# Groups 2 to 7 instead of 2 to 6 of the up-projection in seven products, and the weight sums' transfers in a list that is not emptied ahead of the last gate

## The chip, the cores and the metric

The kernel runs on one core of one Trainium2 chip. The metric is the device time of one execution in microseconds (us). TensorE is called PE here, its weight loads PEld, VectorE DVE, ScalarE ACT, GpSimd POOL and SyncE SP, as in the profile.

## The reference, cut to what matters

The program computes two layers of an encoder trunk for 512 tokens of 1024 channels. Each layer has a mixing half and a feed-forward half:

```
h = rmsnorm(x)                          # per token
proj = h @ w_in                         # gates, convolution branch, three attentions
branch = [y_a, y_b, y_c, y_d] @ w_branch
mixed = sum_n sigmoid(gate_n) * branch_n
x = x + mixed @ w_out
u = depthwise_conv3(rmsnorm(x) @ w_up)  # 1024 -> 2 x 2816
x = x + (silu(u_gate) * u_up) @ w_down  # 2816 -> 1024
```

All arithmetic is float32. The change touches how `@ w_up` is split into products, and when some sums of weights for `@ w_down` and `@ w_up` are made.

## The kernel before, in words

**Float32 products.** Each weight tile of 128x1024 numbers is fetched from HBM to `w_raw` (L248, a DMA on SP's queue), rounded to `w_hi` on ACT (L252), and the rest is put into `w_lo` on DVE (L254). A product of such a pair with a pair `xh`, `xl` takes three matmuls, `w_hi*xh`, `w_hi*xl` and `w_lo*xh` (L273 to L275 in `prod`). A tile that has been fetched and split is a unit. `unit()` asks for units two ahead of the one that it hands out; there are three buffers each for `w_hi` and `w_lo`, and for the units of seven products four for the raw data (two named `w_raw`, two named `w_more`).

**The stages of a layer.** First come the token-major projections of the attentions, with the attentions and the convolution done step by step beside the PE's later products; then the gates of four branches in the order 1, 2, 3, 0 (`gates`, from L839). Each gate has eight blocks of 24 matmuls 128x512 and eight small branch products of 6. After the block of a gate, DVE makes `t` (L849), ACT the tanh (L851), and after the branch product DVE makes another `t` (L878); POOL adds it to the running sum `mx` (L879, for the last gate only for the blocks 0 to 5). In the last gate, branch 0, ACT and DVE then split the sum into `mh` and `ml` (L883, L884) for the product with `w_out`. The tiles `t` share two buffers (tag `t1`), so a third `t` waits until POOL has added the first. After `w_out` comes the feed-forward half: the up-projection (`ffn`), and the down-projection (`down`).

**Seven products.** The 44 blocks of 128 columns of the up-projection form 11 groups (gate and up columns of two neighbouring blocks). A whole group takes four blocks of 24 matmuls 128x512 (L273 to L275). For the groups in `SEVEN` a scheme of Strassen's kind takes seven products of 24 matmuls 128x256 each (L992 in `seven`): A11, A22 and A12 use a quarter of the weights as it is, S1 to S4 use sums of quarters, which the kernel makes itself in DRAM. S4 of a group is issued after the first product of the next group. The down-projection is done in seven products throughout and uses sums of weights too.

**The sums.** Two generators make them with DMAs from POOL's queue, DRAM to DRAM, some of them accumulating: `quarter_sums` (eight transfers of 512 KB for each group in `SEVEN`, L1110 by way of the helper `dma`) and after it `weight_sums` (24 transfers of 1024 or 768 KB for each layer, L1133 by way of `add`). Each of these DMAs waits for the matmul that was issued last when it was emitted (`paced`). They are chained in `slowly`, which makes 12 empty steps first, then one step for each transfer of `quarter_sums` and four for each of `weight_sums`.

**Side work.** `tick()` takes one step of every generator in the list `side`. A block of a gate ticks twice, a product of the seven twice. Ahead of the last gate, `layer` runs `while self.side: self.tick()`: the list is emptied there, with no matmul between the ticks. In the kernel before, the list holds the chain of sums as well. POOL takes its instructions in order, DMA issues and adds alike.

**Splits for the down-projection.** `split_pair` makes from two finished blocks of the up-projection the operands of the seven products of the down-projection. `EARLY` lists after which blocks the first six calls are emitted; the other five are emitted in `down`. The blocks of group 7 are 14 and 15.

Of the kernel before, what the change touches and what calls it, by code (L numbers as in the profile page):

```python
# [34 lines left out]

SLOW = 1

SEVEN = (2, 3, 4, 5, 6)


def up_steps():

    steps, held = [], []
    for g in range(NP2):
        if g in SEVEN:
            own = [('seven', g, n) for n in ('S3', 'A11', 'A22', 'S2', 'A12', 'S1', 'S4')]
        else:
            own = [('whole', 2 * g + i, s) for i in range(2) for s in range(2)]
        steps += own[:1] + held
        held = own[-1:] if g in SEVEN else []  # L50
        steps += own[1:len(own) - len(held)]
# [2 lines left out]

UP_STEPS = up_steps()

EARLY = (14, 15, 16, 18, 19, 20)
EPS = 1e-6
BIG = 1e30
EB = 4  # L60
# [35 lines left out]
def weight_units():  # L96
# [17 lines left out]
    for g in range(NP2):  # L114
        if g in SEVEN:
            units.extend(('quarter', (g, r, c), 1024) for r in range(2) for c in range(2))
# [102 lines left out]
class Trunk:  # L219
# [667 lines left out]
    def tick(self):  # L887

        for g in list(self.side):

            with self.tc.issue_after(self.last_mm.ins):
                r = next(g, 'end')
            if r == 'end':
                self.side.remove(g)
            if r in ('end', 'free') and g is self.head:
                self.head = None
                self.activate()
        return bool(self.side)

    def activate(self):  # L900
# [124 lines left out]
    def conv_part(self, i, s):  # L1025
# [22 lines left out]
        self.F.append(fl)  # L1048
        if i in EARLY:
            self.split_pair(self.F, EARLY.index(i), self.got)  # L1050

# [56 lines left out]
    def quarter_sums(self, l):  # L1108

        dma = lambda *a, **k: self.paced(self.nc.gpsimd.dma_start(*a, **k))  # L1110
        q, t = self.quarters[l], self.qsums[l]
        for g in SEVEN:
            for n in ('S1', 'S2', 'S3', 'S4'):
                t[g, n] = self.dram.tile([P, 1040], F32, name=f"q{n}{g}", tag=f"q{n}{g}", bufs=2)[:, :1024]
        for n, a in (('S3', (1, 0)), ('S1', (1, 1))):
            for g in SEVEN:
                dma(t[g, n], q[(g,) + a])
                yield
        for n, a in (('S3', (0, 0)), ('S1', (1, 0))):
            for g in SEVEN:  # L1120
                dma(t[g, n], q[(g,) + a], accum_op=ALU.add)
# [38 lines left out]
    def pair_tags(self, j):  # L1160
# [4 lines left out]
        late = [(f"lt{n // 2}", n % 2) for n in range(10)]  # L1165
        hi = [f"fh{2 * j}", f"fh{2 * j + 1}"] if j < len(EARLY) else x[2 * (j - len(EARLY)):][:2]
        lo = ["lo", "lo"] if j == 0 else [(f"fp{j - 1}", 0), (f"fp{j - 1}", 1)]
# [9 lines left out]
    def split_pair(self, F, j, got):  # L1177
# [19 lines left out]
        bh, bl = (t[:, (lo, hi)[j % 2]] for t in got['b'])  # L1197
        a = self.fp.tile([P, S], F32, name="sum", tag="xr" if j < len(EARLY) else "fth", bufs=2)

# [16 lines left out]
    def down(self, F, last):  # L1216
# [9 lines left out]

        got, todo = self.got, list(range(len(EARLY), NP2))
        A, B = ([self.mm() for _ in range(2)] for _ in range(2))
# [94 lines left out]
    def run(self):  # L1323
        nc, tc = self.nc, self.tc
        with ExitStack() as st:
# [36 lines left out]
            self.w_emitted = self.w_used = 0  # L1362
            self.first_hi = None
            self.w_ready, self.w_fast = [], 0
            self.side, self.waiting, self.head = [], [], None

            self.cst = self.const.tile([P, NRES], F32, name="cst", tag="cst", bufs=1)
            self.ident = self.cst[:, C_ID:C_ID + P]
# [40 lines left out]
    def layer(self, l):  # L1409
        tc = self.tc  # L1410
        last = l == L - 1
        self.Y, self.mixed, self.MH, self.glu_u = [None] * 4, [], [], []
        with tc.tile_pool(name="gate", bufs=1, reuse_waits="tile") as self.gp:
            with tc.tile_pool(name="attn", bufs=1, reuse_waits="tile") as self.ap:
                self.scratch = lambda: self.gp.tile([P, S], F32, name="raw", tag="t1", bufs=2)
                pss = self.token_major(None, self.aux) if l == 0 else self.early
                Q = self.new_Q()
                for b in range(NB):
                    self.evac_q(Q)(b, pss[b])
                with self.first():  # L1420
                    for _ in self.qk_stats(Q, 4, 4, None):
                        pass
                self.derive_params()
                V = self.new_V()
                self.tabs = [None] * 4
                self.queue(chain(self.na_biases(l, 3 if l else 5), self.qk_norm(Q, 4, 4, 0),
                                 self.attention('na', V, 1)))
                self.side.append(self.slowly(chain(self.quarter_sums(l), self.weight_sums(l))))
                Vd = self.new_V()
                self.project_v(V, Vd)  # L1430
                Q = self.project_qk()
                ready = self.beside(self.qk_stats(Q, 4, 4, 0))
                self.queue(chain(ready, self.qk_norm(Q, 4, 4, 2), self.attention('dil', Vd, 2)))
                self.glu()
                self.side.append(self.conv())
                V = self.new_V()
                Q = self.project_swa(V)
                ready = self.beside(self.qk_stats(Q, 4, 2, 2))
                self.queue(chain(ready, self.qk_norm(Q, 4, 2, 4), self.attention('swa', V, 3)))
                for n in ORDER[:3]:  # L1440
                    self.gates(n)
                while self.side:
                    self.tick()
            with tc.tile_pool(name="outp", bufs=1, reuse_waits="tile") as self.op:
                self.gates(ORDER[3])
                self.xnew = self.new_res()
                self.start_norm('g_ffn')
                for d in range(0, KT, 2):

                    cuts = (0, KT - 2, KT) if d == 0 else (0, KT)  # L1450
                    pss, ws = [self.mm(), self.mm()], []
                    for k0, k1 in zip(cuts, cuts[1:]):
                        for e in range(2):
                            if k0 == 0:
                                ws.append(self.unit())
                            hi, lo = ws[e]
                            for k in range(k0, k1):
                                s = slice(k * P, (k + 1) * P)
                                self.prod(pss[e], hi[:, s], lo[:, s], self.MH[k][0], self.MH[k][1], k == 0,
                                          k == KT - 1)  # L1460
                            if k1 == KT:
                                self.update(d + e, pss[e], self.op)
                self.xres = self.xnew
                self.broadcast_norm()
        if last:
            self.resT = self.dram.tile([S, D], F32, name="resT", tag="resT", bufs=1)
        with tc.tile_pool(name="ffn", bufs=1, reuse_waits="tile") as self.fp:
            self.scratch = lambda: self.fp.tile([P, S], F32, name="raw", tag="cy0", bufs=2)
            F = self.ffn(l, last)
            if last:  # L1470
                self.down(F, True)
                return
            self.load_prm(l + 1)
            self.xnew = self.new_res()
            self.sq_tag = "fth"
            self.start_norm('g_mix')
            self.down(F, False)
            self.finish_norm(5, 8, 4)

            self.early = self.token_major(None, self.aux)  # L1480
            self.xres = self.xnew
            self.sq_tag = "sq"
# [45 lines left out]
```

## Time and profile before

| | us |
|---|---|
| median of 3 runs | 1640.66 (1640.5 to 1641.07) |
| profiled execution, its time | 1639.18 |
| its span, first to last instruction | 1637.4 |
| PE busy | 1541.0 (94%) |
| DVE busy | 1251.0 (76%) |
| ACT busy | 895.8 (55%) |
| POOL busy | 205.4 (13%) |
| mean granted TensorE clock | 0.971 |

The profiled execution lies 1.78 us above its span and 1.48 us below the median. In the profile a time of the trace is counted from the span's start. The two layers look alike; the second starts its last gate some 815 us after the first. A busy PE is the sum of matmuls that overlap: a matmul of 128x512 is shown as 390 ns, but the next starts 227 ns after it.

### The profile page before, as it was taken

Reading aid. Unit: us, or ns where it says so; the run is one execution under the profiler, and the core shown is the slowest. Engines: PE = TensorE matmul, PEld = TensorE weight load, DVE = VectorE, ACT = ScalarE, POOL = GpSimd, SP = SyncE. Lnnn points to the kernel's source line nnn. Section 1 sums busy time; section 2 is a strip of 40 time slices with the busy share of each in tenths; the row PEclk is TensorE's granted clock in tenths of the full one; section 3 lists DMA queues with packets and bytes.
Section 4 is the critical chain, followed back from the end, with each engine's and each line's share of the span. In section 5 each row is a group of like instructions: output and inputs, shape, how many; then the busy total and the mean of one; then the engine's idle time right before and its main releaser. Section 6 shows DMA issues by size and latency. Waiting matters only on the chain.

```text
span 1637.4 us, 21918 instructions
## 1 busy us (share of the span) xinstructions
PE 1541.0 (94%) x7842; PEld 1311.0 (80%) x7842; DVE 1251.0 (76%) x2114; ACT 895.8 (55%) x1504; POOL 205.4 (13%) x308
## 2 busy tenths in 40 slices
PE   9999999990999999999999999999809999999999
PEld 7888888870788998888888888888708889988887
DVE  6699988740669999986576899887306699999964
ACT  6778777320446665464457686763204556655643
POOL 0044122122110000000002231122221000000000
PEclk9999999995999999999999999999959999999999
DMA  7788764599673554356567988645996747753565
GB/s 233 226 232 229 205 173 142 157 204 236 155 265 103 180 185 136 96 182 202 184 183 222 249 224 197 171 158 157 199 231 170 264 119 209 208 157 93 173 221 166
DMA packets 124797, 306.84 MB, mean 187 GB/s; under 512 B 28176, under 2 KB 30096, under 8 KB 124688
## 3 DMA queue, kind: packets, MB, share of 16 engines
q1 hardware_dynamic: 93712, 212.10, 40.8%
q0 software_dynamic: 30688, 92.81, 25.3%
q8 instruction: 62, 1.02, 0.2%
q10 hardware_dynamic: 288, 0.52, 0.1%
q14 instruction: 47, 0.39, 0.1%
HBM read 287.56 MB, written 100.67 MB: 237 GB/s over the span
## 4 chain that ended last, share of the span: by engine, by line
PE 83%; DMA 6%; DVE 4%; ACT 3%; issue 3%; POOL 2%; SPq 0%; POOLq 0%; ACTq 0%; DVEq 0%
PE mm L273 15%; PE mm L274 15%; PE mm L275 15%; PE aux L992 11%; DMA sums<-sums 4%; PE aux L1225 2%; PE aux L1223 2%; PE aux L1224 2%; PE mm L502 2%; PE mm L504 2%; PE mm L503 2%; PE mm L1224 2%; PE mm L1225 2%; PE mm L1223 2%; PE mm L992 2%
## 5 line engine op out<-in xcount | busy, mean ns | idle before, releaser
L252 ACT ACTIVATE w_hi<-w_raw 128x1024 fp32r<-128x1024 f32 (+1 forms) x335 | 350.9, 1047 | 382.1 <-PE mm L274 127.1
L254 DVE TENSOR_TENSOR w_lo<-w_raw,w_hi 128x1024 fp32r<-128x1024 f32 (+1 forms) x335 | 407.3, 1217 | 94.5 <-ACT w_hi L252 92.3
L273 PE MATMUL mm<-xh,w_hi 128*128 128x512 f32 x960 | 377.3, 393 | 89.5 <-DVE t L849 89.5
L275 PE MATMUL mm<-xh,w_lo 128*128 128x512 f32 x960 | 376.1, 392 | 0.0
L274 PE MATMUL mm<-xl,w_hi 128*128 128x512 f32 x960 | 375.9, 392 | 0.0
L273 PEld LDWEIGHTS mm<-xh,w_hi 128*128 128x128 f32 x960 | 181.5, 189 | 126.9 <-ACT w_hi L252 90.3
L275 PEld LDWEIGHTS mm<-xh,w_lo 128*128 128x128 f32 x960 | 181.1, 189 | 39.7 <-DVE w_lo L254 1.1
L274 PEld LDWEIGHTS mm<-xl,w_hi 128*128 128x128 f32 x960 | 181.6, 189 | 36.4
L992 PE MATMUL aux<-form,w_hi 128*128 128x256 f32 x640 | 116.1, 283 | 0.0
L884 DVE SCALAR_TENSOR_TENSOR ml<-mx,mh 128x512 fp32r<-128x512 f32 x16 | 11.0, 690 | 124.0 <-ACT mh L883 123.8
L992 PEld LDWEIGHTS aux<-form,w_hi 128*128 128x128 f32 x640 | 100.0, 192 | 0.2
L440 DVE SCALAR_TENSOR_TENSOR cv<-cv,prm 128x512 f32<-128x512 f32 x120 | 93.7, 780 | 0.7
L992 PE MATMUL aux<-form,w_lo 128*128 128x256 f32 x320 | 90.6, 283 | 0.0
L879 POOL TENSOR_TENSOR mx<-mx,t 128x512 f32<-128x512 f32 x44 | 65.2, 1487 | 156.7 <-DVE t L878 141.8
L883 ACT ACTIVATE mh<-mx 128x512 fp32r<-128x512 f32 x16 | 10.0, 627 | 135.4 <-POOL mx L879 130.9
L502 PE MATMUL mm<-w_hi,xh 128*128 128x512 f32 x192 | 76.4, 398 | 0.4 <-DVE V L630 0.4
L1033 ACT ACTIVATE cy<-U,prm 128x512 f32<-128x512 f32 x88 | 68.7, 807 | 12.7 <-DVE U L1070 7.6
L503 PE MATMUL mm<-w_lo,xh 128*128 128x512 f32 x192 | 75.0, 390 | 0.0
L504 PE MATMUL mm<-w_hi,xl 128*128 128x512 f32 x192 | 74.8, 390 | 0.0
L1110 POOL DMA_DIRECT2D qS<-W x60 | 43.6, 727 | 217.9 <-PE aux L780 107.0
L767 ACT ACTIVATE e<-e,rl 128x256 f32<-128x256 f32 (+2 forms) x96 | 57.3, 597 | 22.2 <-DVE rl L766 21.9
L849 DVE TENSOR_TENSOR t<-mm,RB 128x512 f32<-128x512 f32 x64 | 43.8, 684 | 30.3 <-PE mm L275 30.0
(339 smaller groups left out, 3297.8 us busy)
## 6 DMA issues: line engine op xcount, KB each, us to landing
w_raw<-W SPq DMA_DIRECT2D x213, 512.0 KB, 3.8
qS<-W POOLq DMA_DIRECT2D x60, 512.0 KB, 6.5
sums<-W POOLq DMA_DIRECT2D x24, 1024.0 KB, 12.3
w_raw<-qS SPq DMA_DIRECT2D x40, 512.0 KB, 3.7
w_raw<-W SPq DMA_DIRECT2D x66, 256.0 KB, 3.9
w_raw<-sums SPq DMA_DIRECT2D x44, 256.0 KB, 3.8
w_raw<-sums SPq DMA_DIRECT2D x22, 512.0 KB, 4.6
qS<-qS POOLq DMA_DIRECT2D x20, 512.0 KB, 4.9
```

Of the source, the lines that this page charges most:

```text
L252: w = nc.scalar.activation(hi[:, s], raw[:, s], AF.Copy)
L254: nc.vector.tensor_tensor(lo[:, s], raw[:, s], hi[:, s].bitcast(F32), ALU.subtract)
L273: mm(ps, lhsT=wh, rhs=xh, start=start, stop=False)
L274: mm(ps, lhsT=wh, rhs=xl, start=False, stop=False)
L275: self.last_mm = mm(ps, lhsT=wl, rhs=xh, start=False, stop=stop)
L440: self.after_mm(v.scalar_tensor_tensor(acc, u[:, t:t + S], w(t), acc, ALU.mult, ALU.add))
L502: mm(pss[b], lhsT=self.Xh[k][:, t], rhs=hi[:, s], start=k == 0, stop=False)
L503: mm(pss[b], lhsT=self.Xh[k][:, t], rhs=lo[:, s], start=False, stop=False)
L504: self.last_mm = mm(pss[b], lhsT=self.Xl[k][:, t], rhs=hi[:, s], start=False, stop=k == KT - 1)
L992: self.last_mm = nc.tensor.matmul(o, lhsT=w[:, s], rhs=x, start=start and not (e or j or i), stop=j == 3 and i == 2, skip_group_check=True)
L1033: nc.scalar.activation(y, u[:, 1:513], AF.Identity, scale=w(1), bias=self.par('ffn_conv_b', c))
L1223: mm(ps, lhsT=x[0], rhs=w[0][:, cols], start=start, stop=False, skip_group_check=again)
```

## The change

Three edits:

- `SEVEN` takes group 7 as well. `up_steps`, `weight_units` and `quarter_sums` follow from it: group 7 is done in seven products of 24 matmuls 128x256 in place of four blocks of 24 matmuls 128x512, its weights are packed as quarters, and `quarter_sums` has 48 transfers a layer in place of 40.
- `EARLY` names 15, 16, 17, 18, 19, 20 in place of 14, 15, 16, 18, 19, 20. With group 7 in seven products, blocks 14 and 15 end together, after its S4.
- The chain of sums goes into a list of its own, `slow`. `tick()` takes one step of it each time, but the loop ahead of the last gate looks at `side` alone. The steps that are left then go on with the ticks of the last gate and of the up-projection.

```diff
-SEVEN = (2, 3, 4, 5, 6)
+SEVEN = (2, 3, 4, 5, 6, 7)
...
-EARLY = (14, 15, 16, 18, 19, 20)
+EARLY = (15, 16, 17, 18, 19, 20)
...
             if r in ('end', 'free') and g is self.head:
                 self.head = None
                 self.activate()
+        for g in list(self.slow):
+            if next(g, 'end') == 'end':
+                self.slow.remove(g)
         return bool(self.side)
...
-            self.side, self.waiting, self.head = [], [], None
+            self.side, self.slow, self.waiting, self.head = [], [], [], None
...
-                self.side.append(self.slowly(chain(self.quarter_sums(l), self.weight_sums(l))))
+                self.slow.append(self.slowly(chain(self.quarter_sums(l), self.weight_sums(l))))
```

Lines behind the second edit of `tick` stand three further down in the changed kernel: L992 becomes L995, L1110 L1113, L1133 L1136.

How POOL's queue stands at the last gate of layer 0. Before, from the last two adds of the third gate on (`mx` is the running sum, `sums_` the weight sums of `weight_sums`; rows of 16 transfers follow one another, of which the first eight are shown):

```order
L879 TENSOR_TENSOR mx<-mx,t_3756 128x512
L1133 DMA sums_2682<-W 512x512
L879 TENSOR_TENSOR mx<-mx,t_3766 128x512
L1133 DMA sums_2683<-W 384x512
L1133 DMA sums_2681<-W 512x512
L1133 DMA sums_2682<-W 512x512
L1133 DMA sums_2683<-W 384x512
L1133 DMA sums_2681<-sums_2681 512x512
L1133 DMA sums_2682<-sums_2682 512x512
L1133 DMA sums_2683<-sums_2683 384x512
L1133 DMA sums_2681<-W 512x512
```

The same place in the changed kernel, from the last add of the third gate to the first memset of the up-projection:

```order
L879 TENSOR_TENSOR mx<-mx,t_3776 128x512
L1136 DMA sums_3126<-W 384x512
L1136 DMA sums_3124<-W 512x512
L879 TENSOR_TENSOR mx<-mx,t_3903 128x512
L879 TENSOR_TENSOR mx<-mx,t_3952 128x512
L1136 DMA sums_3125<-W 512x512
L879 TENSOR_TENSOR mx<-mx,t_4002 128x512
L879 TENSOR_TENSOR mx<-mx,t_4051 128x512
L1136 DMA sums_3126<-W 384x512
L879 TENSOR_TENSOR mx<-mx,t_4107 128x512
L879 TENSOR_TENSOR mx<-mx,t_4156 128x512
L1136 DMA sums_3124<-W 512x512
```

Before, 16 transfers stood between the third gate's adds and the first of the last gate's; now two stand ahead of that first add, one after each second add, and one after the last.

Further on in POOL's queue of the changed kernel, behind the loads of `xf` (the residual, for the seven products' own operands) at the start of the up-projection:

```order
L946 DMA xf<-res_4197 128x512
L946 DMA xf<-res_4198 128x512
L1136 DMA sums_3125<-W 512x512
L1136 DMA sums_3126<-W 384x512
L1136 DMA sums_3124<-sums_3124 512x512
L1136 DMA sums_3125<-sums_3125 512x512
L1136 DMA sums_3126<-sums_3126 384x512
```

In the kernel before nothing of the sums stood behind `xf`; now 14 transfers follow it, each waiting for a matmul of the up-projection. The four ticks between two of them are two blocks in the whole groups 0 and 1, and two products in the groups in seven: by the ticks' count three of the 14 fall to the former and 11 to the latter, the last at the first product of group 5.

On PE, layer 0, where the S1 product of the last group in seven ends. Before, this is the end of group 6 (`form` are the operands of S1, `xh_`, `xl_` the normed input) and group 7 follows as blocks of 512 columns:

```order
L992 MATMUL aux<-form,w_hi 128x256 x2
L992 MATMUL aux<-form,w_lo 128x256
L273 MATMUL mm<-xh_4264,w_hi 128x512
L274 MATMUL mm<-xl_4265,w_hi 128x512
L275 MATMUL mm<-xh_4264,w_lo 128x512
```

In the changed kernel the same passage is the end of group 7 and the start of group 8:

```order
L995 MATMUL aux<-form,w_hi 128x256 x2
L995 MATMUL aux<-form,w_lo 128x256
L273 MATMUL mm<-xh_4261,w_hi 128x512
L274 MATMUL mm<-xl_4262,w_hi 128x512
L275 MATMUL mm<-xh_4261,w_lo 128x512
```

Nothing else moves there: the held S4 still follows the first block of the next group.

## The prediction

> **What bounds the kernel now.** The page comes first. PE is busy nearly throughout, so time can come only from where PE stands still, or from fewer matmuls.
>
> ```profile
> PE 1541.0 (94%) x7842; PEld 1311.0 (80%) x7842; DVE 1251.0 (76%) x2114; ACT 895.8 (55%) x1504; POOL 205.4 (13%) x308
> ```
>
> The view of waits, read for PE first, names two waits that hold nearly all of the idle time, then what stood behind them.
>
> ```profile
> ACT mh L883 <- POOL mx L879: 130.9, 10, 55.7
> PE mm L273 <- DVE t L849: 89.5, 2, 45.1
> ```
>
> PE stood 89.5 us in two waits, the longer 45.1 us, so the other 44.4 us: one in each layer. The timeline of PE shows the first, in the last gate (the third number is the idle time ahead of the row and what ended it):
>
> ```profile
> 367.03 0.39 PE L275 MATMUL mm<-yh,w_lo 128*128 128x512 f32 x1
> 412.52 0.76 PE L273 MATMUL mm<-xh,w_hi 128*128 128x512 f32 x1 [45.10 <-DVE t L849]
> ...
> 417.35 0.40 PE L275 MATMUL mm<-xh,w_lo 128*128 128x512 f32 x1
> ...
> 421.69 0.39 PE L273 MATMUL mm<-xh,w_hi 128*128 128x512 f32 x1
> ...
> 427.13 0.39 PE L273 MATMUL mm<-yh,w_hi 128*128 128x512 f32 x1
> ```
>
> DVE's `t` was late because both buffers of `t` held sums that POOL had not added. POOL's timeline tells why it had not:
>
> ```profile
> 338.04 1.65 POOL L879 TENSOR_TENSOR mx<-mx,t 128x512 f32<-128x512 f32 x1
> 339.27 3.41 POOL L1133 DMA_DIRECT2D sums<-W  x3
> 351.42 0.95 POOL L1133 DMA_DIRECT2D sums<-W  x1 [8.74 <-issue]
> ...
> 377.85 1.05 POOL L1133 DMA_DIRECT2D sums<-W  x1 [11.70 <-DMA sums<-sums]
> ...
> 408.15 0.95 POOL L1133 DMA_DIRECT2D sums<-W  x1 [1.25 <-DMA sums<-sums]
> 408.76 1.62 POOL L879 TENSOR_TENSOR mx<-mx,t 128x512 f32<-128x512 f32 x1
> ```
>
> Between two adds, from 339 to 408 us, POOL did nothing but issue the 16 drained transfers, most of them behind the landing of an earlier one. PE ran on for 28 us on blocks that needed no add, then stopped.
>
> **The list that is not emptied.** By the order of POOL's queue, none of the 16 transfers stays in a block ahead of the last gate's adds. The two waits go: 45.1 + 44.4 = 89.5 us. After the wait PE is slow for a while: from 412.52 to 417.35 are eleven starts in 4.83 us, from 417.35 to 421.69 nineteen in 4.34 us. At the later rate eleven take 2.5 us, so each stall costs 2.3 us more, 4.7 us in both layers. Removed: 94.2 us.
>
> What is late next in the last gate? Each transfer left among the adds waits for a matmul that lies before the branch product its next add waits for, so it is issued by then. POOL needs 1 us for it, beside adds that come every 5 us (its row at 408.76 and the next, below). After the stall the old kernel ran the rest of this gate and on to `w_out` with PE never idle:
>
> ```profile
> 414.25 1.28 POOL L879 TENSOR_TENSOR mx<-mx,t 128x512 f32<-128x512 f32 x1 [3.86 <-DVE t L878]
> ```
> ```profile
> 413.00:438.00 25.00, 25.00 (x102) 20.08 (x101) 15.55 (x21) 10.42 (x14) 6.13 (x5) 0.92 0.71 174
> 330.00:367.00 37.00, 37.00 (x165) 30.64 (x164) 14.64 (x15) 8.52 (x10) 10.78 (x12) 1.00 0.99 210
> ```
>
> (The last two are stretches: busy us of PE, PEld, DVE, ACT, POOL, granted clock, DMA share, GB/s.) The second matters as well: with the DMA engines at 0.99 of their time, sums running, PE lost nothing beside a gate's demand for weights. So I take all of the 94.2 us.
>
> **Group 7 in seven products.** One block of 24 matmuls of 512 columns runs from 421.69 to 427.13, 5.44 us; a whole group is four, 21.76 us. The chain of waits gives the seven's rate:
>
> ```profile
> 540.06 17.28 PE aux L992 x144
> ```
>
> That is 120 ns each, and 7 x 24 of them 20.16 us. The group saves 1.60 us, two layers 3.2 us, although it has an eighth fewer columns: half the width costs more than half the time. The Trainium skill, in TensorE: Matmul & The Clock Gate, section Back-to-back issue gap, gives a warm gap of N/2.4 + 2.5 ns for N columns. By that the saving would be 2.4 us a group (estimate from the page), 1.5 us more in the sum; the trace disagrees at both widths (227 and 120 ns), so its rows stand.
>
> The eight more quarter transfers a layer are issued among the gates (before, POOL had 60 with 0.7 us each at L1110); they push the weight sums 8 ticks later. The stretch at 0.99 above is their cover; without it, the price would be 8 x 0.7 = 6 us of POOL in a layer, on an engine that PE waits for only through `mx`. I cost them at nothing.
>
> **What the moved transfers meet: the DMA engines.** Eleven of the 14 transfers behind `xf` fall beside the groups in seven. Two views of that stage and one of a stretch in which both queues were full:
>
> ```profile
> 525.00:629.00 104.00, 104.00 (x845) 102.93 (x844) 99.02 (x131) 68.27 (x90) 0.00 (x0) 1.00 0.55 178
> ...
> 629.00:716.00 87.00, 87.00 (x397) 72.52 (x396) 79.57 (x123) 46.59 (x66) 0.00 (x0) 1.00 0.31 98
> ```
> ```profile
> q0 software_dynamic: 30688, 92.81, 25.3%
> ```
> ```profile
> q0 software_dynamic: 263, 0.52, 55.6%
> q1 hardware_dynamic: 250, 0.96, 50.9%
> ```
>
> The weights take 0.55 of the engines there. POOL's queue q0 moved 92.81 MB in 25.3% of 1637 us, 4.5 us of all engines for 1 MB; a mean transfer (two of 1024 KB and one of 768) has 0.96 MB, so 4.3 us. One is issued every two products, 5.76 us, in which the weights need 3.2: together 7.5, more than there is. Eleven need 47 us, the weights 67 of the stage's new 121 us, 114 in all: the backlog clears about when the stage ends, and the blocks behind leave 0.69 of the engines free. So for some 100 us weights and sums share full engines. The last rows are such a stretch (357 to 362 us): each queue had half, and q1 moved 0.96 MB in 5 us, or 2.7 us for a unit of 0.52 MB. A product lasts 2.88 us. By that row nothing is lost.
>
> The other end comes from landing times and buffers.
>
> ```profile
> DMA to landing us min/median/max: 6.9/9.0/10.1
> ```
> ```profile
> w_raw<-qS SPq DMA_DIRECT2D x40, 512.0 KB, 3.7
> ```
> ```profile
> L252 ACT ACTIVATE w_hi<-w_raw 128x1024 fp32r<-128x1024 f32 (+1 forms) x335 | 350.9, 1047 | 382.1 <-PE mm L274 127.1
> L254 DVE TENSOR_TENSOR w_lo<-w_raw,w_hi 128x1024 fp32r<-128x1024 f32 (+1 forms) x335 | 407.3, 1217 | 94.5 <-ACT w_hi L252 92.3
> ```
>
> A weight landed in 6.9 to 10.1 us beside the drained sums (339 to 357 us) against 3.7 us alone. With four raw buffers, one turns once in four products, 11.5 us; less 1.05 and 1.22 us for the two splits, 9.2 us are left for a landing. The median fits, the worst does not: at 10.1 us a turn takes 12.4 us, 7.5% more, over 100 us some 7.5 us a layer. So 0 to 15 us in all; less than nothing is excluded, as more traffic frees no buffer. I take 4 us, near the row that has both queues full at the needed rate, for the starts of accumulating transfers.
>
> **The tail: DVE.** The stretch from 629 to 716 us above is groups 7 to 10, in which DVE has 7.4 us to spare. Group 7 as a whole group takes of DVE four times L254 and four times the first three rows here, twice the last:
>
> ```profile
> L1035 DVE SCALAR_TENSOR_TENSOR cy<-U,prm,cy 128x512 f32<-128x512 f32 x88 | 65.0, 745 | 0.3
> L1034 DVE SCALAR_TENSOR_TENSOR cy<-U,prm,cy 128x512 f32<-128x512 f32 x88 | 64.2, 747 | 2.1 <-ACT cy L1033 2.1
> L1070 DVE TENSOR_TENSOR U<-mm,RB 128x512 f32<-128x512 f32 x48 | 32.6, 683 | 9.1 <-PE mm L275 8.9
> L1047 DVE TENSOR_TENSOR f<-cy,fth 128x512 f32<-128x512 f32 x44 | 29.8, 680 | 0.1
> ```
>
> That is 4 x 3.39 + 2 x 0.68 = 14.9 us. Without it DVE has 64.7 us of work in 65.2 us of PE time, for `EARLY` still puts six splits there. Cover is the four PSUM banks of the blocks, three blocks or 16 us of delay. At best the tail costs nothing; at worst the spare that is lost, 7.4 - 0.5 = 6.9 us a layer, shows up at the start of `down`. A gain is excluded, since work of DVE is only packed closer. I take 1 us a layer, near nothing since PE has lost nothing in the groups in seven, where DVE is busy 99.02 of 104 us: 2 us.
>
> **The sum.** Against the profiled 1639.2 us: 94.2 + 3.2 - 4 - 2 = 91.4 us less, 1547.8 us. The median lies 1.5 us above the profiled time, so 1549 us. With nothing lost it is 1543 us, with both worst ends 15 + 14 us lost, 1572 us.
>
> **The rivals.** *A, each accumulating transfer holds weights off for a time of its own.* In the trace weights issued just after such a transfer began landed at the worst 10.1 us, 6.4 us later than the usual 3.7. Six of the eleven accumulate. If their delays hit PE one by one, a layer loses 6 x 6.4 = 38 us; if the buffers hide half, 19 us. Time: 1549 + 2 x 19 - 4 = 1583 us. For it speaks that row; against it the stretch at 0.99, where PE lost nothing, though a gate wants a unit only every 6.8 us or so. The Trainium skill speaks for it: DMA: Bandwidth & Descriptors, section Queues, rings and completion order, says that an engine drains a whole packet of up to 64 descriptors from one ring before it goes to the next. The trace half disagrees, as both queues had half of the engines from 357 to 362 us.
>
> *B, sums go first throughout (the other side).* Place: products of groups 2 to 6. Mechanism: while a transfer of sums is in flight the weights get nothing, PE runs out of units and stands, and the sums thus take PE's time as they did before, only later. Landings of the drained sums in the longest stretch:
>
> ```profile
> DMA to landing us min/median/max: 7.6/16.6/29.8
> ```
>
> The 29.8 us is with four in flight, 7.45 us each; eleven of them 82 us a layer. Time: 1640.7 - 97.4 + 164 = 1707 us. It decides from 97.4 / 22 = 4.4 us a transfer on, about its share of all engines (4.3 us). Against it: q1's half from 357 to 362 us.
>
> *C, the gate stays shut.* POOL takes its queue in order, and three transfers lie between adds of the last gate. If one must wait for a landing, POOL stands as before. The longest such wait:
>
> ```profile
> POOL sums L1133 <- DMA sums<-sums: 41.2, 12, 12.9
> ```
>
> Three of 12.9 us are 39 of the 45 us of a layer: 1549 + 78 = 1627 us. Against it: these transfers add to sums whose first copies were issued 24 ticks earlier, one and a half gates.
>
> **How the numbers follow.** The forecast gets 0.78: the stall's cause and price are read from rows, and the two costs set against it are bounded. A gets 0.13, C 0.05, B 0.04. Its own bounds are 1543 and 1572 us; 1541 to 1574 us adds 2 us at either end for another execution's spread, and with the low part of A it holds 8 in 10. A measurement of this kernel tells about 0.2%, 3 us, from no change. Faster by more: all but B and a trace of C, 0.95; within it 0.01; slower 0.04.
>
> **What would show it.** Right: the wait of PE for `t` (L849) is gone in both layers, and so is the half clock after it; the adds (L879) of the last gate come every 5 to 7 us; seven products count 2 x 168 matmuls more at 120 ns; PE has no idle between the last gate and the end of `down`; q0 is busy from 525 us less 47 on, beside PE's products. Wrong: waits of ACT's `w_hi` for `w_raw` followed by idle PE in the seven products (A, B), waits of POOL in the last gate for a landing (C), or waits of PE for `w_lo` or `U` after group 7 (the tail). If the wait for `t` goes and the time is still over 1574 us, the DMA term was sized wrongly.

## The result, and the profile after

| | before | after |
|---|---|---|
| median, us | 1640.58 (4 runs) | 1583.02 (4 runs) |
| span of the profiled execution, us | 1637.4 | 1581.1 |
| mean granted clock | 0.971 | 0.988 |

The ratio is 0.9653, 95% interval 0.9636 to 0.9671: faster by 57.6 us, where the prediction said 91.4 and its range ended at 1574 us. The page shows PE busier, but not full:

```profile
PE 1540.1 (97%) x7986; PEld 1319.0 (83%) x7986; DVE 1260.4 (80%) x2126; ACT 905.5 (57%) x1516; POOL 217.4 (14%) x324
```

The view of waits (total us, times, longest) answers to the two lines of before. `mh` is down from 130.9 to 29.6 us, PE's wait for `t` is gone, and two other waits of PE have come, with their forerunners on POOL, ACT and DVE:

```profile
POOL sums L1136 <- DVE xl L336: 93.1, 2, 46.5
...
ACT mh L883 <- POOL mx L879: 29.6, 11, 2.7
...
ACT xf L953 <- DMA xf<-res: 24.2, 2, 12.1
DVE forms L958 <- ACT xf L953: 23.5, 2, 11.8
...
PE mm L273 <- DVE U L1073: 20.6, 2, 10.3
...
PE aux L995 <- ACT sv L1007: 13.2, 2, 7.8
```

PE's idle time went from 89.5 to 33.8 us. The stretches (busy us of PE, PEld, DVE, ACT, POOL, granted clock, DMA share, GB/s) say where it is not: the last gate and `w_out` of the first layer (the first two), its seven products, and its groups 8 to 10:

```profile
330.00:367.00 37.00, 37.00 (x165) 30.65 (x164) 17.53 (x21) 11.87 (x15) 10.47 (x9) 1.00 0.55 150
367.00:413.00 46.00, 46.00 (x204) 38.09 (x204) 28.17 (x35) 18.73 (x26) 6.92 (x5) 1.00 0.66 175
479.00:600.00 121.00, 121.00 (x966) 119.01 (x964) 114.92 (x152) 80.79 (x106) 9.84 (x12) 1.00 0.91 271
612.00:670.00 58.00, 58.00 (x269) 48.51 (x268) 57.98 (x94) 32.30 (x44) 0.00 (x0) 1.00 0.33 101
```

Where the time went is plainer from PE's timeline, as the time between the first matmuls of three stages (us; in the changed kernel's first layer they start at 391.09, 490.45 and 676.73):

| | before, first layer | before, last | changed, first layer | changed, last |
|---|---|---|---|---|
| up to `w_out` (last layer: from `down` of the first) | 438.0 | 539.8 | 391.1 | 492.0 |
| `w_out` to the seven products | 87.5 | 87.5 | 99.4 | 99.7 |
| seven products to `down` | 187.9 | 187.9 | 186.3 | 203.6 |

The first row has the gates and is 94.7 us shorter in both layers together. The second has lost 24.1 us, and the third has gained 1.6 us in the first layer and lost 15.7 in the last.

**First place: the start of the up-projection, in both layers.** PE's timeline, around the gap:

```profile
456.59 0.39 PE L275 MATMUL mm<-xh,w_lo 128*128 128x512 f32 x1
467.26 0.77 PE L273 MATMUL mm<-xh,w_hi 128*128 128x512 f32 x1 [10.29 <-DVE U L1073]
467.83 0.63 PE L274 MATMUL mm<-xl,w_hi 128*128 128x512 f32 x1
```

DVE's timeline at that place. Between the first Newton step for `RB` (L307) and the next (L308), DVE waits for an `xf` to make `forms` from; `U`, which PE's banks wait for, needs `RB`:

```profile
442.44 0.42 DVE L307 TENSOR_SCALAR rs_i<-ms 128x512 int32<-128x512 int32 x1
454.58 0.43 DVE L958 TENSOR_TENSOR forms<-xf 128x256 f32<-128x256 f32 x1 [11.72 <-ACT xf L953]
454.93 0.42 DVE L308 TENSOR_SCALAR RB<-rs_i 128x512 int32<-128x512 int32 x1
...
466.43 1.28 DVE L1073 TENSOR_TENSOR U<-mm,RB 128x512 f32<-128x512 f32 x2
```

POOL's timeline shows why `xf` is late. One transfer of sums stands ahead of all eight loads. It waits for a matmul of the first block of the up-projection: that block begins at 434.61 us, and its tick halfway through emits the transfer (the view names DVE's `xl`, which ended at about the same time). The loads go out in a burst behind it:

```profile
437.92 1.03 POOL L1136 DMA_DIRECT2D sums<-W  x1 [46.53 <-DVE xl L336]
...
438.70 4.25 POOL L946 DMA_DIRECT2D xf<-res  x7
452.76 0.54 POOL L946 DMA_DIRECT2D xf<-res  x1 [9.82 <-DMA sums<-W]
```

In the program's text the loads come first: `ffn` calls `seven_forms`, which emits them, ahead of that block. The scheduler has put the transfer ahead of them in POOL's queue, and POOL takes its queue in order.

The landing times of the eight `xf` loads, in this kernel and then in the one before, where they went out one by one, nearly all during `w_out` (450.8 to 485.0 us):

```profile
DMA to landing us min/median/max: 5.3/14.7/15.2
```
```profile
DMA to landing us min/median/max: 3.3/3.9/5.7
```

**Second place: the seven products of the last layer, and only there.** The weights' issues on SP's queue and their landings, in the first layer (479 to 600 us) and in the last (1255 to 1376 us); the three numbers of the issue are least, median and longest ns:

```profile
L248 SPq DMA_DIRECT2D w_raw<-qS x22: 319/326/327, 487.4 to 597.6; - x22
DMA to landing us min/median/max: 3.4/7.7/9.4
```
```profile
L248 SPq DMA_DIRECT2D w_raw<-qS x19: 319/326/6064, 1265.4 to 1371.9; - x19
DMA to landing us min/median/max: 3.4/6.9/17.7
```

The median is no higher, but single weights land after 17.7 us. PE meets them by way of ACT, which copies a bank of PE to `sv` (L1007) behind the `w_hi` that waits for the weight; here are ACT and then PE at the longer of the two stalls:

```profile
1346.62 1.06 ACT L252 ACTIVATE w_hi<-w_raw 128x1024 fp32r<-128x1024 f32 x1 [5.95 <-DMA w_raw<-qS]
...
1351.12 1.06 ACT L252 ACTIVATE w_hi<-w_raw 128x1024 fp32r<-128x1024 f32 x1 [1.51 <-DMA w_raw<-W]
1352.08 0.58 ACT L1007 ACTIVATE sv<-aux 128x512 f32<-128x512 f32 x1
```
```profile
1352.71 0.80 PE L995 MATMUL aux<-form,w_hi 128*128 128x256 f32 x2 [7.76 <-ACT sv L1007]
```

What the last layer alone has there is `turn_res`: for each of eight tiles it loads the residual (`xr`, 256 KB), transposes it on DVE and writes it to `resT` in four transfers of 64 KB, in pieces of 128 bytes, all on the weights' queue.

### The profile page after: what moved, and what is told of

Its sections match the earlier page's. It is cut to its first block, busy times and chain, and to the rows that moved or that the text cites. A ratio compares the mean times of both kernels' runs of the same rounds, so it can differ in the third digit from the quotient of the medians.

```text
span 1581.1 us, 22330 instructions
## 1 busy us (share of the span) xinstructions
PE 1540.1 (97%) x7986; PEld 1319.0 (83%) x7986; DVE 1260.4 (80%) x2126; ACT 905.5 (57%) x1516; POOL 217.4 (14%) x324
## 4 chain that ended last, share of the span: by engine, by line
PE 80%; issue 7%; DVE 5%; DMA 4%; ACT 3%; POOL 0%; SPq 0%; ACTq 0%; POOLq 0%; DVEq 0%
PE mm L273 13%; PE mm L274 13%; PE mm L275 13%; PE aux L995 12%; PE aux L1227 3%; PE aux L1226 3%; PE aux L1228 3%; PE mm L502 2%; PE mm L504 2%; PE mm L503 2%; DMA w_raw<-W 2%; PE mm L1227 2%; PE mm L1228 2%; PE mm L1226 2%; DMA xf<-res 2%
## 5 line engine op out<-in xcount | busy, mean ns | idle before, releaser
L273 PE MATMUL mm<-xh,w_hi 128*128 128x512 f32 x896 | 351.8, 393 | 20.6 <-DVE U L1073 20.6
L274 PE MATMUL mm<-xl,w_hi 128*128 128x512 f32 x896 | 350.4, 391 | 0.0
L275 PE MATMUL mm<-xh,w_lo 128*128 128x512 f32 x896 | 350.1, 391 | 0.0
L273 PEld LDWEIGHTS mm<-xh,w_hi 128*128 128x128 f32 x896 | 169.0, 189 | 55.6 <-issue 21.4
L274 PEld LDWEIGHTS mm<-xl,w_hi 128*128 128x128 f32 x896 | 169.1, 189 | 33.6
L995 PE MATMUL aux<-form,w_hi 128*128 128x256 f32 x768 | 143.1, 288 | 13.2 <-ACT sv L1007 13.2
L995 PEld LDWEIGHTS aux<-form,w_hi 128*128 128x128 f32 x768 | 122.9, 197 | 13.8 <-ACT sv L1007 13.7
L995 PE MATMUL aux<-form,w_lo 128*128 128x256 f32 x384 | 110.2, 287 | 0.0
L1113 POOL DMA_DIRECT2D qS<-W x72 | 52.2, 726 | 218.2 <-PE aux L780 98.8
L995 PEld LDWEIGHTS aux<-form,w_lo 128*128 128x128 f32 x384 | 75.4, 196 | 0.0
L767 ACT ACTIVATE e<-e,rl 128x256 f32<-128x256 f32 (+2 forms) x96 | 57.3, 597 | 21.9 <-DVE rl L766 21.4
L1136 POOL DMA_DIRECT2D sums<-W x36 | 31.8, 883 | 251.6 <-DVE xl L336 93.1
```

The costliest lines, as they stand in the source:

```text
L273: mm(ps, lhsT=wh, rhs=xh, start=start, stop=False)
L274: mm(ps, lhsT=wh, rhs=xl, start=False, stop=False)
L275: self.last_mm = mm(ps, lhsT=wl, rhs=xh, start=False, stop=stop)
L995: self.last_mm = nc.tensor.matmul(o, lhsT=w[:, s], rhs=x, start=start and not (e or j or i), stop=j == 3 and i == 2, skip_group_check=True)
```

## The experiments

Theory Q: the transfer of sums ahead of the `xf` loads costs the first place. Theory T (at first P): the turned residual, beside the sums, costs the second. Lines of the experiments' kernels stand up to three further down. The kernel "xf first" of the third experiment is the base of most that follow.

### The list alone, and group 7 alone

First the changed kernel with both tables of before:

```diff
-SEVEN = (2, 3, 4, 5, 6, 7)
-EARLY = (15, 16, 17, 18, 19, 20)
+SEVEN = (2, 3, 4, 5, 6)
+EARLY = (14, 15, 16, 18, 19, 20)
```

> Only the list that is not emptied; group 7 stays whole (five groups in seven products, the old list of early splits). The prediction's theory gives group 7 as 1.6 us a layer, so 1583.0 + 3.2 = 1586 us. The place of the sums in POOL's queue is the same as in the changed kernel (one of them, of 768 KB now, ahead of the xf loads), so PE's two waits of some 10 us for U stay. Rival: the sixth group is what overloads the DMA engines or DVE in the seven products (eight more quarter transfers, packed splits). Then without it PE's waits in the last layer's seven products (13.2 us) go too, and the time is 1586 - 15 = 1571 us, below the changed kernel.

Measured: 1586.03 us, 0.9681 (0.9664 to 0.9697), 3.0 us above the changed kernel. The rival falls: PE still waits in the last layer's seven products, 8.9 us of it for `sv`.

The other half was the kernel before with both new tables and the chain of sums still in `side`.

> Only group 7 in seven products; the sums' list is emptied ahead of the last gate as before. By the prediction's theory the products save 3.2 us, but eight more quarter transfers a layer stand ahead of the weight sums, so that two more of these are drained at the gate (18 in place of 16). 69 us of POOL for 16 drained transfers is 4.3 us each, so two more lengthen each layer's stall by 8.6 us: 1640.6 - 3.2 + 17 = 1654 us, slower. Rival: the length of the stall is set by the DMA engines' whole backlog and not by the count, and two more cost nothing: 1637 us.

Measured: 1642.77 us, 1.0020 (1.0010 to 1.0029): some 2 us slower, neither the 1654 us expected nor the rival's 1637. Its wait of PE:

```profile
PE mm L273 <- DVE t L849: 95.9, 2, 48.9
```

The drained stalls grew by 95.9 - 89.5 = 6.4 us for four more transfers, 1.6 us each and not 4.3. From the first of the seven products to `down` PE takes 186.28 us here and 187.88 in the kernel before, in both layers, with no wait in either: group 7 saves 1.60 us a layer. The rest of the gain is the list's.

### The xf loads first

```diff
-        for g in list(self.slow):
+        self.ticks += 1
+        for g in list(self.slow) if self.ticks > self.held else []:
...
         self.side.append(work())        # end of seven_forms
+        self.held = self.ticks + 1
```

> The changed kernel with one step of the sums' list skipped after the loads of xf are emitted. In POOL's queue the one transfer of sums that stood ahead of the eight xf loads then stands behind them; every other row keeps its order. Theory Q (the queue's order): the xf loads waited for the first up-block's matmul only because this transfer stood ahead of them; without that they go out as each residual tile lands, PE's two waits for U (10.3 us each) and the 1.4 us of slow clock after each go, 1583 - 23.4 = 1560 us. Rival S (sharing): the xf loads land late because weights and sums fill the DMA engines, whatever the order; then they land in 12 to 15 us as in the changed kernel, and the time stays within 5 us of it, 1578 to 1583 us. Rival V (DVE): the forms' own work on DVE ahead of the first U is what holds PE; the gain is then less than half, 1571 us or more.

Measured: 1564.28 us, 0.9542 (0.9528 to 0.9556): 18.7 us less than the changed kernel. POOL's timeline now has the loads one by one behind their residual tiles (from 403.8 us on), and the transfer behind them; its last load and the transfer:

```profile
437.98 0.54 POOL L947 DMA_DIRECT2D xf<-res  x1 [4.49 <-DMA res<-xn]
440.58 1.08 POOL L1138 DMA_DIRECT2D sums<-W  x1 [2.07 <-PE aux L363]
```

The loads' landings, and then PE's waits:

```profile
DMA to landing us min/median/max: 3.4/3.8/6.1
```
```profile
PE aux L996 <- ACT sv L1008: 16.7, 3, 7.7
...
PE mm L273 <- DVE U L1075: 0.7, 1, 0.7
```

Q holds, S and V fall: the wait for `U` went from 20.6 to 0.7 us. 4.7 us of the expected 23.4 are missing; 3.5 of them are the second place, whose wait grew from 13.2 to 16.7 us. So the 18.7 us are what is left of a first place worth 24.1 us after the second has grown: from the seven products to `down` the last layer takes 207.8 us here and 203.6 in the changed kernel.

### Half the pace alone

```diff
-                yield 4
+                yield 2
```
(at each of the four places in `weight_sums`)

> The changed kernel with one weight sum in two ticks in place of four and nothing else. As in the changed kernel one transfer of sums stands ahead of the xf loads in POOL's queue (it is now a copy from the sums themselves), and no sums fall beside the seven products. Theory Q (the transfer ahead of the xf loads costs 18.7 us, as the run with the xf loads first said): 1541.1 + 18.7 = 1560 us, with PE's two waits for U in place. Rival D: the xf loads are late only when many more transfers are still to come behind them; then nothing is lost, 1541 us.

Measured: 1561.94 us, 0.9517 (0.9501 to 0.9533). A second test of Q, in which no sums are issued beside the seven products at all. POOL and PE show the same picture with a copy, `sums<-sums`, in front:

```profile
438.23 0.68 POOL L1136 DMA_DIRECT2D sums<-sums  x1 [46.26 <-DVE xl L336]
...
439.02 3.79 POOL L946 DMA_DIRECT2D xf<-res  x7
```
```profile
PE mm L273 <- DVE U L1073: 14.9, 2, 8.3
```

One transfer in the wrong place of one queue is 21 us here, against the run below that also has the `xf` loads first (1541.05 us).

### Whole rows in place of small pieces

```diff
-        rows = self.resT.rearrange("(i a) c -> a i c", a=32)
+        rows = self.resT[d * S // KT:(d + 1) * S // KT].rearrange("a (h c) -> (a h) c", h=2)
         for q in range(4):
-            nc.sync.dma_start(rows[:, :, d * P + 32 * q:d * P + 32 * q + 32],
-                              xn[32 * q:32 * q + 32].rearrange("a (i b) -> a i b", b=32))
+            nc.sync.dma_start(rows[32 * q:32 * q + 32], xn[32 * q:32 * q + 32])
```

> The changed kernel; in the last layer the turned residual tiles are written as rows of 2 KB in place of pieces of 128 bytes, the same bytes at the same moments and on the same queue (so the rows of the residual stand in the wrong places and the output is not the reference's). Theory P (pieces): in the last layer the weights of the seven products landed in 13.8 to 17.7 us, against 7 to 9.4 us in the first layer, because the many small pieces take the DMA engines; without them PE's waits of 13.2 us for sv and the slow clock after them go, 1583 - 15 = 1568 us. Rival N (not the pieces): the last layer's waits come from the sums, the bytes of the residual, or from the first wait of the stage pushing the sums against the groups in seven; then the time stays at 1580 to 1583 us.

Measured: 1583.41 us, 0.9660 (0.9646 to 0.9675): no change. Issues no longer stall (longest 0.70 us in place of 6.06), but weights still land late, and PE still waits in that stage (7.2 us for `sv`, 3.8 for `w_lo`):

```profile
L248 SPq DMA_DIRECT2D w_raw<-qS x20: 319/338/704, 1255.4 to 1373.7; - x20
...
DMA to landing us min/median/max: 3.4/8.3/16.2
```

P falls: the size of the pieces does not decide the time. That left the residual's bytes on that queue, and the sums alone.

### The residual late: a try that moved half of it, and one that moved it all

```diff
+TURN = {11: (0,), 13: (1, 2), 15: (3,), 17: (4, 5), 19: (6,), 21: (7,)}
...
-        if self.last and i % 2 == 1 and i // 2 < KT:
-            self.turn_res(i // 2)
+        if self.last:
+            for d in TURN.get(i, ()):
+                self.turn_res(d)
```

> The kernel with the xf loads first (1564.3 us), and the last layer's turned residual (eight loads of 256 KB, eight times four writes of 64 KB, all on SP's queue) done behind the blocks 11 to 21 in place of 1 to 15, so after the last of the weight sums has been issued. Theory T: it is this traffic on the queue of the weights, beside the sums, that makes the last layer's weights late; the piece size did not matter. PE's 16.7 us of idle in the seven products and about 1.4 us of slow clock after each of three stalls go: 1564.3 - 16.7 - 4 = 1544 us. Rival L: the last layer is late for another reason (the sums alone): no change, 1564 us. Rival M: the loads and writes collide with the whole groups or with the down-projection, and PE waits there: between 1550 and 1564 us, with the waits behind group 7.

Measured: 1565.57 us, 0.9539 (0.9525 to 0.9553), the time of its base. It does not speak against T: DVE's timeline has four of the eight transposes still among the sums, one of them being

```profile
1298.51 0.71 DVE L1087 STREAM_TRANSPOSE xn<-xr 128x512 f32<-128x512 f32 x1 [6.14 <-DMA xr<-res]
```

The scheduler had put them forward, since nothing in the data held them back. The next run holds them back, with the table `TURN` above and the loads paced in POOL's queue:

```diff
-        nc.sync.dma_start(xr, self.xres[d])
+        self.paced(nc.gpsimd.dma_start(xr, self.xres[d]))
```

> The kernel with the xf loads first (1564.3 us). In the run meant to move the turned residual late, four of its eight tiles had been moved ahead again by the scheduler, into the same seven products. Here its loads stand in POOL's queue behind the last weight sum, each waiting for the matmul before it, so none of its loads, transposes and writes can meet the sums. Theory T (the residual on the queue of the weights, beside the sums, makes the last layer's weights late): PE's idle time in the last layer's seven products goes, 1564.3 - 16.7 - 4 = 1544 us, and the weights there land in 7 to 10 us as in the first layer. Rival L (the last layer's sums do it without the residual): the waits stay, 1560 to 1566 us.

Measured: 1542.88 us, 0.9406 (0.9385 to 0.9428): 21.4 us less than its base. The transposes, the weights in the last layer's seven products (1236 to 1357 us), and PE's longest waits:

```profile
L1087 DVE STREAM_TRANSPOSE xn<-xr x8: 673/703/705, 1339.6 to 1439.2; 128x512 f32<-128x512 f32 x8
```
```profile
DMA to landing us min/median/max: 3.5/7.6/9.4
```
```profile
PE mm L274 <- DVE U L1077: 1.5, 1, 1.5
PE aux L997 <- ACT sv L1009: 1.5, 2, 0.8
```

With the same sums beside the same products, weights land as in the first layer, and PE's 16.7 us for `sv` are down to 1.5. L falls: it is the residual beside the sums. Whether its place on the weights' queue matters, as T has it, this run can't tell; the next two bear on it.

### The residual on POOL's queue, whole and in part

The first run has both edits, the second that of the writes alone; `turn_res` stands where it stood.

```diff
-        nc.sync.dma_start(xr, self.xres[d])
+        nc.gpsimd.dma_start(xr, self.xres[d])
...
-            nc.sync.dma_start(rows[:, :, d * P + 32 * q:d * P + 32 * q + 32],
+            nc.gpsimd.dma_start(rows[:, :, d * P + 32 * q:d * P + 32 * q + 32],
```

> The kernel with the xf loads first (1564.3 us); the turned residual's loads and writes at the same places, but on POOL's queue with the sums in place of SP's queue with the weights. Theory H (a half for each queue): the weights are late since the residual takes from the share of their own queue. Then the weights land in 7 to 10 us as in the first layer, PE's 16.7 us go, and the sums end later: 1544 to 1550 us. Rival E (the engines' total): what counts is the work of all DMA engines, whichever queue brings it; then the waits stay, 1560 to 1566 us. Rival O (order): the sums behind the residual in POOL's queue are held up by the transposes that the writes wait for, and units of the down-projection wait for sums: over 1566 us.

Measured: 1566.35 us, 0.9545 (0.9531 to 0.9560). The weights' landings (1255 to 1335 us) and what PE and DVE waited for (1240 to 1350 us):

```profile
DMA to landing us min/median/max: 6.6/8.3/9.7
```
```profile
DVE xn L1085 <- DMA xr<-res: 23.0, 4, 10.1
...
PE aux L996 <- DVE w_lo L254: 16.0, 3, 7.8
```

H is right on the weights and wrong on the time: off their queue the residual no longer delays them, but its loads wait among the sums, and DVE, which takes its work in order, stands before a transpose while `w_lo` waits behind it. E gave 1560 to 1566 us, but its weights were to stay late, and they do not. O gave over 1566 us by another way: POOL does stand for transposes, but what PE waits for is DVE, not a unit of the down-projection. So T holds: weights come late only where the residual is on their own queue while sums run on the other.

> The kernel with the xf loads first (1564.3 us); the turned residual's eight loads of 256 KB stay on SP's queue at their places, its 32 writes of 64 KB go to POOL's queue among the sums. In the run with both on POOL's queue the weights landed in at most 9.7 us, but DVE stood 23.0 us for the residual's loads, which lay behind sums. Theory W (the writes on the weights' queue are what makes the weights late): weights land in at most 10 us, DVE no longer waits for the loads, PE's 16.7 us go: 1544 us, with 2 to 5 us more if transposes wait for a buffer that a write behind a sum still holds. Rival R (the loads of 256 KB do it): weights still land in 15 us and more now and then, 1555 to 1564 us.

Measured: 1559.52 us, 0.9510 (0.9490 to 0.9529), between W and R. The weights land in up to 13.8 us with the loads alone in their queue, and a transpose now waits for a buffer that a write still holds:

```profile
DVE xn L1085 <- DMA resT<-xn: 10.4, 2, 8.9
```
```profile
DMA to landing us min/median/max: 3.4/8.5/13.8
```

PE waits 7.0 us for a `w_lo` behind that transpose, and 2.8 for `sv` in place of 16.7. So the loads alone still make weights late (13.8 us, against 9.4 without the residual and 18.9 with all of it), but how the 21.4 us split between loads and writes stays open, as the moved writes cost PE time in another way.

### Half the pace with the xf loads first

The edits of "xf first" and `yield 2`; then these with the table `TURN` as well.

> The kernel with the xf loads first (1564.3 us), and one weight sum in two ticks in place of four: 18 of the 24 transfers then stand ahead of the xf loads and six go out beside the whole groups 0 and 1, none beside the seven products. Theory T and the sums' contention both say that PE's waits in the last layer's seven products go, since the turned residual then meets no sums: 1564.3 - 16.7 - 4 = 1544 us. Rival C of the prediction, here at twice the pace: in the last gate one transfer for each block of 6.8 us takes longer than that beside the weights, an accumulating transfer has to wait for the landing of its first copy, POOL stands and PE waits for t again; with 3 to 13 us for each of three such waits and layer it is 1544 + 18 to 78, 1562 to 1622 us.

Measured: 1541.05 us, 0.9389 (0.9373 to 0.9404), the fastest. Rival C is tested at its hardest, with a transfer at each block of the last gate; the stretches there, and the page:

```profile
330.00:367.00 37.00, 37.00 (x165) 30.65 (x164) 17.82 (x22) 12.54 (x16) 13.35 (x12) 1.00 0.99 243
367.00:400.00 33.00, 33.00 (x147) 27.31 (x146) 19.01 (x24) 11.75 (x16) 9.21 (x11) 1.00 0.87 204
```
```profile
PE 1532.5 (100%) x7986; PEld 1312.9 (85%) x7986; DVE 1259.3 (82%) x2126; ACT 904.5 (59%) x1516; POOL 218.9 (14%) x324
```

PE is busy throughout, with the DMA engines at up to 0.99 of their time beside it, and in the view of waits POOL never waits there for a landing of sums.

> Both: the xf loads first, the turned residual late, one weight sum in two ticks. If each of the two parts alone removes the last layer's waits, both together give no more than one: 1544 us. If half the pace costs in the last gate (rival C), it shows here as the difference to the run with the late residual alone.

Measured: 1541.12 us, 0.9390 (0.9376 to 0.9404). Nothing is left to gain by moving the residual once no sums run beside it.

## Why the prediction was wrong, point by point

**The stalls (94.2 us): right.** Waits for `t` and the slow clock behind them are gone in both layers, and the stretches up to `w_out` are 94.7 us shorter. But four new stalls, two in each of the new places, brought slow clock back: after the gap at 467.26 us, PE's rows are 0.77 and 0.63 us long in place of 0.39.

**"What is late next in the last gate?" Right for the gate, and stopped there: the first step that failed.** The gate loses nothing, not even at twice the pace. The step priced the moved transfers against POOL's adds alone, and leaned on the old kernel's idle-free run on to `w_out`. The new order of POOL's queue, quoted before the prediction, had a transfer that is held for a matmul of the up-projection ahead of the `xf` loads, which in the old kernel overlapped `w_out`. It cost 24.1 us between `w_out` and the seven products; taking that one transfer out of the way gained 18.7 us, 20.9 at half the pace. The term was missing altogether, and "PE has no idle between the last gate and the end of `down`" with it.

**Group 7 (3.2 us): right.** 1.60 us in each layer of the run with group 7 alone. The 3.0 us between the list alone and the whole change agree, though other waits differ between those two as well.

**The DMA engines (4 us, bounds 0 to 15): the second step that failed.** It was worked out for the first layer and doubled. There it is nothing: weights beside sums land in up to 9.4 us, where the prediction had 9.2 us to spare for a landing, and PE is full from 479 to 600 us. In the last layer the seven products lose 17.3 us in the changed kernel (203.6 us in place of 186.3), and 21.4 us is what moving the residual gains once the first place is gone: some two to three times the worst end of 7.5 us for a layer. The residual's own loads and writes share the weights' queue there, and the step did not ask what the last layer adds to it. Without them 1.0 us is lost there (187.3 us). The queues' bytes in a stretch beside accumulating sums, with the residual (the "xf first" kernel, 1260 to 1284 us) and without it (its loads behind the sums, 1262 to 1280 us):

```profile
q0 software_dynamic: 1569, 3.28, 70.6%
q1 hardware_dynamic: 3416, 3.27, 44.8%
```
```profile
q0 software_dynamic: 912, 1.99, 58.6%
q1 hardware_dynamic: 843, 3.11, 46.7%
```

With the residual q1 moved 3.27 MB in 24 us, 136 GB/s, the residual's own among them; without it 3.11 MB in 18 us, 173 GB/s, nearly all weights. A unit in 2.88 us needs 182. The Trainium skill (DMA: Bandwidth & Descriptors, Queues, rings and completion order) says that an engine takes turns between the queues by whole packets. The rows fit that and do not show it: the profile counts each piece of 128 bytes as a packet (2760 packets of the first stretch are under 512 bytes), so q1 has 142 in a microsecond in place of 47, and it moved fewer bytes. The run with whole rows lost as much in another way: there q1 moved 4.75 MB in 27 us (1283 to 1310 us), 176 GB/s, but nine writes and two loads of the residual were issued in that stretch, 1.1 MB, which leaves the weights some 135 GB/s (an estimate from these rows). So pieces slow the queue and bytes take from it; which of the two counts for how much is not shown.

**The tail (2 us): nothing.** From 612 to 670 us DVE is busy 57.98 of 58.00 us and PE 58.00: DVE is full, and PE's banks cover it.

**The sum.** With every term of cost at nothing it gave 1543 us. The kernel with both causes taken away measures 1542.88, and the fastest 1541.05. What it removed was sized well; what it set against that was sought in the wrong places.

**The rivals.** A gave 1583 us, and 1583.02 came, but not by A: six accumulating transfers a layer run beside the first layer's products, land in up to 25.7 us there, and hold no weight off so long that PE waits. That the number came is luck: an agreeing number is no proof of a mechanism. B and C did not appear.

## What to carry to other kernels

When work moves along an in-order queue, price everything that the moved item comes to stand ahead of, up to the end of its new stretch, not only the wait that it left; an item paced to a later matmul takes every load behind it along. Read that order from the queue as it is built, for a scheduler may change the program's. Price shared queues in each layer by that layer's own traffic: a last layer with an extra output step is another kernel. And before an experiment is read, see in its trace that the work moved: it may have been put back.

## What the runs showed that was not expected

- An issue of a weight on SP's queue, 0.32 us as a rule, took up to 6.06 us in the changed kernel, where writes in pieces of 128 bytes stood in the same queue, and 0.70 at most with rows of 2 KB.
- Four transposes of 0.70 us each held DVE for 23.0 us before their loads had landed, and that cost PE 16.0 us: DVE takes its work in order, so a short instruction costs what it waits for.
- The residual on the weights' queue made the sums on the other queue faster, not slower. Accumulating transfers of 1024 KB landed after 18.6 us (median of four) in the last layer's seven products without the residual there, after 13.0 with it (the kernels of the two pairs of rows above, 1255 to 1376 us); in the first layer, which has no residual to turn, they take 18.5 (479 to 600 us).
